# One table of attention biases for four heads, with the slope carried by the queries

## The chip, the cores and the metric

The kernel runs on one core of one Trainium2 chip. The metric is device time in microseconds (us), the median of several runs. Engines: PE is TensorE (PEld its weight loads), DVE VectorE, ACT ScalarE, POOL GpSimd, SP the engine whose queue issues every DMA of this kernel.

## The reference, cut to what matters

One layer of a hybrid decoder trunk: RMSNorm, one input projection to 13 slices of 256 columns, four token mixers side by side (dilated attention, spatial gating, pooling, retention), gates, one output projection, a second RMSNorm and the residual. Sequence 2048, width 1024, float32. The change touches the attention mixer: four heads of 64 channels, each with three branches of dilation 1, 4 and 16. A query sees itself and 128 earlier positions at the branch's step.

```python
def _alibi_slopes(n):
    return jnp.exp2(-8.0 * (jnp.arange(n, dtype=jnp.float32) + 1.0) / n)
...
    scores = jnp.einsum('bhrnqd,bhrnkd->bhrnqk', qb, kc).astype(jnp.float32) * (hd ** -0.5)
...
    band = (dist >= 0) & (dist <= window // dil)
...
    bias = -slopes[:, None, None, None, None] * (dist * dil).astype(jnp.float32)
    scores = jnp.where(mask, scores + bias, -jnp.inf)
```

With four heads the slopes are 1/4, 1/16, 1/64 and 1/256. The three branches are joined with weights from their softmax denominators.

## The kernel before, in words

**First part (lines 144 to 528).** Two halves of 1024 tokens. Each half normalises and transposes its tokens, then goes through the 13 slices. Every float32 operand is split into a high and a low part of type float32r, and each product takes three matmuls. `weights(col, n)` loads the columns of one slice (L245, tile `raw`, two buffers), copies them to the high part on ACT (L246) and subtracts that from `raw` on DVE or POOL for the low part (L247). For n = 128 it makes one copy and one subtraction of 128x1024; three such weights can be alive. `a_qk(0, e, gs)` projects the queries of head pair e and writes both parts to DRAM (`qk_d`); it runs for e = 0 and 1 in each half, so four times.

**Attention (lines 547 to 710).** `attention(0)` does heads 0 and 1, `attention(1)` heads 2 and 3. A head loads its queries `q2` and its keys `k2a`, `k2b` (L557 to L561), its bias table `tab` (L562, L563: 128x640 float32, 320 KB, one buffer) and, per branch, values `att_v` (L570 to L575). These tiles of 2048 columns share seven buffers of the tag `m8`; `tab` has one of its own. The branches come in the order 4, 16, 1. A branch takes blocks of 128 queries: two matmuls per block into `ps_s` (L626, L627), one DVE instruction that adds the table, scales and takes the row's minimum of the negated scores (L632), the exponential on ACT with the row sum (L634), transposes on PE into `ps_pt`, a split into high and low (L641 ACT, L642 DVE), two matmuls with the values into `ps_o`, and the sum of the two halves of that bank (L656 ACT, L657 DVE). At a branch's end its row statistics go to DRAM; after a head's third branch `weigh(h)` reads them back and writes the branches' weights (`fd`).

```python
            tab = pm.tile([P, T_HEAD], F32, tag="tab", bufs=1, name="tab")
            D.dma_start(tab, catt[:, h * T_HEAD:(h + 1) * T_HEAD])
...
                V.tensor_tensor_reduce(out=pr[:, u, :w], in0=ps[:, u, :w], in1=bb, scale=-(HD ** -0.5), scalar=3e38,
                                       op0=ALU.add, op1=ALU.min, accum_out=neg)
```

**Beside and after it.** `combine(0)` reads the weights of heads 0 and 1 (`fb`, L756), multiplies and adds the branches on DVE and POOL (L759 to L763) and stores the result; it stands in program order between the two calls of `attention`. Nine `partial(t)` tiles multiply the other three mixers by their output weights (`ps_out`, 36 matmuls each) while `attention(1)` and its surroundings run; `tc.issue_after` sets the earliest place of each. Then `combine(1)` and sixteen `final(t)` tiles: the rest of the output projection, norm, residual, store.

**What sets the order.** The program is traced in the order of the code. A planner then simulates it with estimated costs and writes out each engine's instruction order once, before the launch; on the chip each engine keeps to that order and waits where an input is late. SP's queue is one of these orders.

Of the kernel before, what the change touches and what calls it, by code (L numbers as in the profile page):

```python
# [9 lines left out]
F32 = mybir.dt.float32  # L10
# [3 lines left out]
AF = mybir.ActivationFunctionType  # L14
ALU = mybir.AluOpType
# [3 lines left out]
P = 128  # L19
# [6 lines left out]
HD = 64  # L26
# [4 lines left out]
COL = {n: i * 256 for i, n in enumerate(  # L31
    ("aq", "ak", "av", "ag", "bu", "bv", "bg", "cx", "cg", "dq", "dk", "dv", "dg"))}

C_ID, C_DEC, C_ZETA, C_XI, C_CD, C_INVP, C_CNT, C_MIX = 0, 128, 640, 896, 1152, 1408, 1410, 1442
T_1, T_4, T_16, T_HEAD = 0, 256, 512, 640
MASKED = 1e30
PB = {"part": 1, "fin": 8}
# [29 lines left out]
def attention_tables():  # L67

    f = np.float32
    tab = np.zeros((P, 4, T_HEAD), f)  # L70
    pos = np.arange(P)
    p1 = 16 * (pos % 8) + pos // 8
    p4 = 4 * (8 * (pos // 32) + pos % 8) + (pos // 8) % 4
    c4 = 4 * (pos % 32) + pos // 32
    k1 = np.concatenate([c4, P + c4])
    k4 = np.arange(2 * P)
    slopes = np.exp2(f(-8.0) * (np.arange(4, dtype=f) + f(1.0)) / f(4.0)).astype(f)
    for h in range(4):
        for off, qi, ki, dil in ((T_1, p1, k1, 1), (T_4, p4, k4, 4), (T_16, pos, P + pos, 16)):
            dist = qi[:, None] + P - ki[None, :]  # L80
            band = (dist >= 0) & (dist <= P)
            tab[:, h, off:off + len(ki)] = np.where(band, -slopes[h] * f(HD ** 0.5) * (dist * dil).astype(f), f(-MASKED))
    return tab.reshape(P, 4 * T_HEAD)


@with_exitstack
def hymba(ctx: ExitStack, tc: tile.TileContext, x, pre_g, w_in, sgu_g, sgu_w, sgu_b, pool_w,
# [4 lines left out]
    def r32(ap):  # L92
        return ap.bitcast(F32)
# [50 lines left out]
    with ExitStack() as c1:  # L144
# [88 lines left out]

        w_src = w_in[0].rearrange("(k p) e -> p k e", p=P)

        def weights(col, n, eng=V):

            if n == P:
                w = p1.tile([P, 2, KT, n], F32R, tag="w128", bufs=3, name="w128")
            else:  # L240
                w = pa.tile([P, 2, KT, n], F32R, tag="w256", bufs=1, name="w256")
            kc = KT * P // n
            for k in range(0, KT, kc):
                raw = p1.tile([P, kc, n], F32, tag="raw", bufs=2, name="raw")
                D.dma_start(raw, w_src[:, k:k + kc, col:col + n])  # L245
                A.activation(w[:, 0, k:k + kc], raw, AF.Copy)  # L246
                eng.tensor_tensor(w[:, 1, k:k + kc], raw, r32(w[:, 0, k:k + kc]), ALU.subtract)  # L247
            return w

        def proj_t(w, g):  # L250
# [52 lines left out]
                                    r32(vt[:, j]).rearrange("p h l d -> p h (l d)"))  # L303

        def a_qk(which, e, gs):
            w = weights(COL["aq" if which == 0 else "ak"] + e * P, P)
            for g in gs:
                ps = proj_t(w, g)
                hl = p1.tile([P, 2, GRP], F32R, tag="ys", bufs=2, name="qk_s")
                if which == 0:  # L310
                    ps, hi, lo = by_token(ps), blocked(hl[:, 0]), blocked(hl[:, 1])
                else:
                    ps, hi, lo = ps.rearrange("p (t c) -> p t c", c=4), by_chain(hl[:, 0]), by_chain(hl[:, 1])
                A.activation(hi, ps, AF.Copy)
                V.tensor_tensor(lo, ps, r32(hi), ALU.subtract)
                D.dma_start(qk_d[which][e][:, :, g * GRP:(g + 1) * GRP], r32(hl))
# [227 lines left out]

    marks = []

    def attention(p):
        o01 = (big if p == 0 else po).tile([P, 2, SEQ], F32, tag="big" if p == 0 else "o01", name="att_o01")
        o = [o01[:, 0], o01[:, 1], po.tile([P, SEQ], F32, tag="o2", name="att_o2")]
        for s in range(2):  # L550
            h = 2 * p + s
            rows = slice(s * HD, (s + 1) * HD)
            other = slice((1 - s) * HD, (2 - s) * HD)
            q2 = pm.tile([P, SEQ], F32R, tag="m8", bufs=7, name="q2")
            k2a = pm.tile([P, SEQ], F32R, tag="m8", bufs=7, name="k2a")
            k2b = pm.tile([P, SEQ], F32R, tag="m8", bufs=7, name="k2b")
            D.dma_start(r32(q2[rows]), qk_d[0][p][rows, 0])  # L557
            D.dma_start(r32(q2[other]), qk_d[0][p][rows, 1])
            for z in (rows, other):
                D.dma_start(r32(k2a[z]), qk_d[1][p][rows, 0])  # L560
                D.dma_start(r32(k2b[z]), qk_d[1][p][rows, 1])  # L561
            tab = pm.tile([P, T_HEAD], F32, tag="tab", bufs=1, name="tab")  # L562
            D.dma_start(tab, catt[:, h * T_HEAD:(h + 1) * T_HEAD])  # L563
            for b, dil in enumerate(DILS):
                vt = pm.tile([P, 16, 2 * HD], F32R, tag="m8", bufs=7, name="att_v")
                dst = r32(vt)
                if dil == 1:
                    src = v_d[h].rearrange("(n t c) d -> c t n d", c=4, t=32)
                    for c in range(4):
                        D.dma_start(dst[c * 32:(c + 1) * 32], src[c])  # L570
                elif dil == 4:
                    D.dma_start(dst.rearrange("q (j c) d -> q j (c d)", j=4),
                                v_d[h].rearrange("(j q c) d -> q j (c d)", j=4, c=4))
                else:
                    D.dma_start(dst.rearrange("q r d -> q (r d)"), v_d[h].rearrange("(q r) d -> q (r d)", r=16))  # L575
                qb = q2
                if dil != 1:
                    qb = pm.tile([P, SEQ], F32R, tag="m8", bufs=7, name="q2b")
                    if dil == 4:
                        src = r32(q2).rearrange("p (j k c i) -> p c j k i", j=4, c=4, i=8)  # L580
                        dst = qb.rearrange("p (j c k i) -> p c j k i", j=4, c=4, i=8)
                        for c in range(4):
                            (V if c < 3 else G).tensor_copy(dst[:, c], src[:, c])
                    else:
                        V.tensor_copy(qb.rearrange("p (r w i) -> p r w i", r=16, i=8),
                                      r32(q2).rearrange("p (w r i) -> p r w i", r=16, i=8))
                st = p2.tile([P, 2, 16], F32, tag="stat", bufs=2, name="att_st")
                branch(s, dil, qb, k2a, k2b, vt, tab, o[b], st)
                keep_stats(h, b, dil, st)
            weigh(h)  # L590
        return o

    def branch(s, dil, q2, k2a, k2b, vt, tab, o, st):
        rows = slice(s * HD, (s + 1) * HD)
        other = slice((1 - s) * HD, (2 - s) * HD)
        if dil == 1:
# [20 lines left out]
        def probs(blocks):  # L617

            nb = len(blocks)
            ps = ps2.tile([P, nb, GRP // nb], F32, tag="s", bufs=N_S, name="ps_s")  # L620
            pr = p2.tile([P, nb, GRP // nb], F32, tag="pr", bufs=B_PR, name="att_p")
            res = []
            for u, (n, prev) in enumerate(blocks):
                w = (1 + prev) * P
                qs = slice(n * P, (n + 1) * P)
                mm(ps[:, u, :w], q2[:, qs], keys(k2a, n, prev), True, False)  # L626
                mm(ps[:, u, :w], q2[:, qs], keys(k2b, n, prev), False, True)  # L627
            for u, (n, prev) in enumerate(blocks):
                w = (1 + prev) * P
                bb = bias if dil == 16 or prev else bias[:, P:]  # L630
                neg = st[:, 0, n:n + 1]
                V.tensor_tensor_reduce(out=pr[:, u, :w], in0=ps[:, u, :w], in1=bb, scale=-(HD ** -0.5), scalar=3e38,  # L632
                                       op0=ALU.add, op1=ALU.min, accum_out=neg)
                A.activation(pr[:, u, :w], pr[:, u, :w], AF.Exp, bias=neg, scale=-1.0, accum_out=st[:, 1, n:n + 1])  # L634
                res.append(pr[:, u, :w])
            return res
# [32 lines left out]
        if dil == 16:  # L669
            for n in range(0, 16, 4):  # L670
# [4 lines left out]
                hi, lo = split(pt, GRP)  # L675
# [171 lines left out]
    with ExitStack() as c2:  # L847
        pm = c2.enter_context(tc.tile_pool(name="pm", bufs=1, reuse_waits="tile"))
        p2 = c2.enter_context(tc.tile_pool(name="p2", bufs=1, reuse_waits="tile"))
        ps2 = c2.enter_context(tc.tile_pool(name="ps2", bufs=2, space=PSUM, reuse_waits="tile"))  # L850
        o = attention(0)
        for i in (1, 2, 3):
            out_weights(i, V if i == 2 else G)
        combine(0, o, p2, 2, False, 256, range(0, SEQ, 256))
        o = attention(1)
        for t in range(npart):
            with tc.issue_after(marks[int(len(marks) * (t + spread[0]) / npart * spread[1])]):
                partial(t)
        out_weights(0, G)
# [45 lines left out]
```

## Time and profile before

| | |
|---|---|
| median of 3 runs | 1071.59 us |
| range of the runs | 1070.7 to 1071.6 us |
| the profiled execution: its own time | 1067.77 us |
| span of that execution's profile | 1066.1 us |
| PE busy | 991.5 us, 93% of the span |
| mean granted PE clock, share of full speed | 0.972 |
| first to last instruction on `tab` (L632) | 679.2 to 917.0 us |

The span runs from the first to the last instruction of one execution; the times in the rows count from its start. Busy time is the sum of an engine's instructions; matmuls overlap, so a busy PE is not PE at its peak. A number in square brackets at the end of a timeline row is the idle time of that engine just before, and what ended it.

### The profile page before, as it was taken

The numbers are of one execution on the slowest core, as the hardware profiler recorded it, in microseconds if no ns is written. First come the engines' busy times: TensorE is split into PE (matmuls) and PEld (weight loads), VectorE is DVE, ScalarE is ACT, GpSimd is POOL, SyncE is SP. The second block draws the span as 40 slices with busy tenths as digits, with TensorE's granted clock in tenths as the row PEclk, the third lists the DMA queues.
The fourth block names the chain that finished last, engine by engine and source line by source line (L and its number), as shares of the span: only waits on it lengthen the run. The fifth ranks groups of instructions, "written<-read, shape, count | busy, mean of one in ns | idle before, by whom it ended". The sixth has DMA issues, their size and how long they took to land.

```text
span 1066.1 us, 15681 instructions
## 1 busy us (share of the span) xinstructions
PE 991.5 (93%) x5916; PEld 855.1 (80%) x5916; DVE 532.9 (50%) x1543; ACT 379.7 (36%) x847; POOL 189.6 (18%) x195
## 2 busy tenths in 40 slices
PE   5999999999999999999999999979998889987992
PEld 5889898988877988989897877868987769865781
DVE  7611216696332421023763321467676557627887
ACT  6320222131222420222211111698875548703231
POOL 2310012211232000002220124112114341222000
PEclk9999999999999999999999999989999899998996
DMA  7530313233223331142211930585656963484876
GB/s 275 150 99 21 101 58 115 84 120 95 83 79 99 99 100 40 29 129 80 80 41 50 235 97 29 152 215 150 153 172 141 222 204 78 130 248 114 271 255 218
DMA packets 120394, 136.26 MB, mean 128 GB/s; under 512 B 14976, under 2 KB 96000, under 8 KB 118272
## 3 DMA queue, kind: packets, MB, share of 16 engines
q1 hardware_dynamic: 120320, 135.28, 43.2%
q8 instruction: 46, 0.75, 0.3%
q14 instruction: 28, 0.23, 0.1%
HBM read 98.78 MB, written 36.47 MB: 127 GB/s over the span
## 4 chain that ended last, share of the span: by engine, by line
PE 70%; DMA 15%; DVE 8%; issue 3%; ACT 2%; SPq 1%; POOL 1%; DVEq 0%; ACTq 0%
PE ps_t L96 38%; PE ps_m L96 15%; PE ps_out L96 4%; DMA fb<-fd 4%; PE ps_s L96 3%; PE ps_o L96 3%; PE ps_pt L99 2%; DMA tab<-in_catt_dram 2%; PE ps_of L96 2%; DMA out_dram<-z 2%; DMA z<-partd 2%; DMA cm<-in_cmix_dram 1%; DMA partd<-z 1%; PE ps_in L96 1%; DMA ya<-ya 1%
## 5 line engine op out<-in xcount | busy, mean ns | idle before, releaser
L96 PE MATMUL ps_t<-hh,w 128*128 128x512 f32 x1152 | 368.9, 397 | 0.0
L96 PEld LDWEIGHTS ps_t<-hh,w 128*128 128x128 f32 x1152 | 216.2, 188 | 48.9 <-issue 3.4
L96 PE MATMUL ps_t<-hl,w 128*128 128x512 f32 x576 | 227.0, 394 | 0.0
L96 PE MATMUL ps_m<-w,hh 128*128 128x256 f32 x1024 | 183.6, 282 | 2.4 <-ACT hh L231 2.4
L96 PEld LDWEIGHTS ps_m<-w,hh 128*128 128x128 f32 x1024 | 157.5, 190 | 4.4 <-ACT hh L231 3.4
L96 PE MATMUL ps_out<-wo,yt 128*128 128x512 f32 x576 | 150.9, 408 | 3.7 <-DVE z L829 2.2
L96 PE MATMUL ps_m<-w,hl 128*128 128x256 f32 x512 | 145.5, 284 | 0.2 <-DVE hl L232 0.2
L96 PEld LDWEIGHTS ps_out<-wo,yt 128*128 128x128 f32 x576 | 108.4, 195 | 26.9 <-issue 3.9
L247 DVE TENSOR_TENSOR w<-raw,w 128x1024 fp32r<-128x1024 f32 x46 | 63.5, 1386 | 132.6 <-ACT w L246 132.5
L96 PEld LDWEIGHTS ps_t<-hl,w 128*128 128x128 f32 x576 | 108.4, 188 | 24.1 <-issue 1.4
L96 PEld LDWEIGHTS ps_m<-w,hl 128*128 128x128 f32 x512 | 97.8, 191 | 0.8 <-DVE hl L232 0.4
L634 ACT ACTIVATE att_p<-att_p,att_st 128x128 f32<-128x128 f32 (+1 forms) x192 | 86.5, 453 | 32.0 <-DVE att_st L632 31.7
L246 ACT ACTIVATE w<-raw 128x1024 fp32r<-128x1024 f32 x52 | 54.7, 1059 | 70.2 <-PE ps_t L96 37.6
L632 DVE CUSTOM_DVE_ANT_0 att_p<-ps_s,tab 128x128 f32<-128x128 f32 (+1 forms) x192 | 60.5, 358 | 31.4 <-PE ps_s L96 22.5
L96 PE MATMUL ps_o<-pt_lo,att_v 128*128 128x128 f32 (+1 forms) x204 | 53.9, 300 | 7.2 <-DVE pt_lo L642 7.1
L99 PE MATMUL ps_pt<-ident,att_p 128*128 128x128 f32 x300 | 53.7, 290 | 4.4 <-ACT att_p L634 4.3
L96 PE MATMUL ps_o<-pt_hi,att_v 128*128 128x128 f32 (+1 forms) x204 | 54.4, 288 | 2.4 <-DVE att_o L657 1.9
L642 DVE TENSOR_TENSOR pt_lo<-ps_pt,pt_hi 128x512 fp32r<-128x512 f32 x80 | 51.4, 651 | 5.5 <-ACT pt_hi L641 4.5
L96 PEld LDWEIGHTS ps_o<-pt_lo,att_v 128*128 128x128 f32 x204 | 41.2, 203 | 10.3 <-DVE pt_lo L642 9.5
L641 ACT ACTIVATE pt_hi<-ps_pt 128x512 fp32r<-128x512 f32 x80 | 44.3, 564 | 5.3 <-PE ps_o L96 3.4
L96 PEld LDWEIGHTS ps_o<-pt_hi,att_v 128*128 128x128 f32 x204 | 41.4, 203 | 4.8 <-issue 1.4
L657 DVE TENSOR_TENSOR att_o<-ps_o,att_o 64x512 f32<-64x512 f32 x48 | 32.9, 685 | 20.0 <-ACT att_o L656 19.5
(159 smaller groups left out, 1311.8 us busy)
## 6 DMA issues: line engine op xcount, KB each, us to landing
raw<-in_w_in_dram SPq DMA_DIRECT2D x52, 512.0 KB
qk<-qk_s SPq DMA_DIRECT2D x16, 512.0 KB
att_v<-vd SPq DMA_DIRECT2D x8, 1024.0 KB
xr<-in_x_dram SPq DMA_DIRECT2D x16, 512.0 KB
out_dram<-z SPq DMA_DIRECT2D x15, 512.0 KB
xt<-in_x_dram SPq DMA_DIRECT2D x7, 1024.0 KB
yraw<-yb SPq DMA_DIRECT2D x16, 384.0 KB
partd<-z SPq DMA_DIRECT2D x9, 512.0 KB
```

The source lines that it names most:

```text
L96: return T.matmul(o, lhsT, rhs, start=start, stop=stop, skip_group_check=True)
L99: T.transpose(o, i, ident[:n, :n])
L246: A.activation(w[:, 0, k:k + kc], raw, AF.Copy)
L247: eng.tensor_tensor(w[:, 1, k:k + kc], raw, r32(w[:, 0, k:k + kc]), ALU.subtract)
L632: V.tensor_tensor_reduce(out=pr[:, u, :w], in0=ps[:, u, :w], in1=bb, scale=-(HD ** -0.5), scalar=3e38, op0=ALU.add, op1=ALU.min, accum_out ...
L634: A.activation(pr[:, u, :w], pr[:, u, :w], AF.Exp, bias=neg, scale=-1.0, accum_out=st[:, 1, n:n + 1])
L641: A.activation(hi, pt[:, :w], AF.Copy)
L642: V.tensor_tensor(lo, pt[:, :w], r32(hi), ALU.subtract)
L657: V.tensor_tensor(dst, b0, dst, ALU.add)
```

## The change

The table is built once for slope 1 (128x640 instead of 128x2560 in DRAM) and loaded once, ahead of `attention(0)`. The query weights of head h are multiplied by the inverse of its slope (4, 16, 64 or 256), so that `ps_s` holds the scores divided by the slope; the scale of L632 becomes the slope times the old one. All factors are powers of two. In `weights`, the two heads of a pair have different factors, so the copy and the subtraction are done for each half of the columns: two ACT copies and two DVE `scalar_tensor_tensor` of 128x512 (eight runs of 64 columns) instead of one of each of 128x1024. `branch` gets the head's number instead of its place in the pair.

```diff
+SLOPES = tuple(2.0 ** -(2 * (h + 1)) for h in range(4))
...
-            tab[:, h, off:off + len(ki)] = np.where(band, -slopes[h] * f(HD ** 0.5) * (dist * dil).astype(f), f(-MASKED))
+        tab[:, off:off + len(ki)] = np.where(band, -f(HD ** 0.5) * (dist * dil).astype(f), f(-MASKED))
...
-        def weights(col, n, eng=V):
+        def weights(col, n, eng=V, scales=(1.0,)):
...
-                A.activation(w[:, 0, k:k + kc], raw, AF.Copy)
-                eng.tensor_tensor(w[:, 1, k:k + kc], raw, r32(w[:, 0, k:k + kc]), ALU.subtract)
+                for i, sc in enumerate(scales):
+                    cs = slice(i * n // len(scales), (i + 1) * n // len(scales))
+                    hi, lo = w[:, 0, k:k + kc, cs], w[:, 1, k:k + kc, cs]
+                    A.activation(hi, raw[:, :, cs], AF.Copy, scale=sc)
+                    if sc == 1.0:
+                        eng.tensor_tensor(lo, raw[:, :, cs], r32(hi), ALU.subtract)
+                    else:
+                        V.scalar_tensor_tensor(lo, raw[:, :, cs], sc, r32(hi), ALU.mult, ALU.subtract)
...
-            w = weights(COL["aq" if which == 0 else "ak"] + e * P, P)
+            if which == 0:
+                w = weights(COL["aq"] + e * P, P, scales=[1.0 / SLOPES[2 * e + s] for s in range(2)])
+            else:
+                w = weights(COL["ak"] + e * P, P)
...
-    def attention(p):
+    def attention(p, tab):
...
-            tab = pm.tile([P, T_HEAD], F32, tag="tab", bufs=1, name="tab")
-            D.dma_start(tab, catt[:, h * T_HEAD:(h + 1) * T_HEAD])
...
-                V.tensor_tensor_reduce(out=pr[:, u, :w], in0=ps[:, u, :w], in1=bb, scale=-(HD ** -0.5), scalar=3e38,
+                V.tensor_tensor_reduce(out=pr[:, u, :w], in0=ps[:, u, :w], in1=bb, scale=-SLOPES[h] * HD ** -0.5, scalar=3e38,
...
-        o = attention(0)
+        tab = pm.tile([P, T_HEAD], F32, name="tab")
+        D.dma_start(tab, catt)
+        o = attention(0, tab)
...
-        o = attention(1)
+        o = attention(1, tab)
```

## Rows read from the trace of the kernel before

**Rows 1.** The page's engine totals, and its chain that ended last, by line.

```profile
PE 991.5 (93%) x5916; PEld 855.1 (80%) x5916; DVE 532.9 (50%) x1543; ACT 379.7 (36%) x847; POOL 189.6 (18%) x195
PE ps_t L96 38%; PE ps_m L96 15%; PE ps_out L96 4%; DMA fb<-fd 4%; PE ps_s L96 3%; PE ps_o L96 3%; PE ps_pt L99 2%; DMA tab<-in_catt_dram 2%; PE ps_of L96 2%; DMA out_dram<-z 2%; DMA z<-partd 2%; DMA cm<-in_cmix_dram 1%; DMA partd<-z 1%; PE ps_in L96 1%; DMA ya<-ya 1%
```

**Rows 2.** Windows: length, PE, PEld, DVE, ACT, POOL busy (count), PEclk, DMA share, GB/s.

```profile
700.00:726.00 26.00, 18.27 (x111) 16.68 (x111) 16.05 (x50) 22.11 (x67) 0.61 (x1) 0.74 0.80 216
...
776.00:800.00 24.00, 22.07 (x154) 20.00 (x153) 16.74 (x57) 17.33 (x51) 4.08 (x4) 1.00 0.51 162
...
844.00:874.00 30.00, 21.48 (x97) 17.47 (x98) 16.22 (x52) 11.44 (x37) 12.08 (x15) 0.83 0.79 240
874.00:922.00 48.00, 47.68 (x335) 43.70 (x334) 37.89 (x125) 40.51 (x122) 6.81 (x9) 1.00 0.29 80
```

**Rows 3.** SP's queue in order of time: start, duration, line, transfer.

```profile
593.08 0.59 SPq L563 DMA_DIRECT2D tab<-in_catt_dram  x1
...
604.27 0.37 SPq L245 DMA_DIRECT2D raw<-in_w_in_dram  x1
...
775.29 0.34 SPq L563 DMA_DIRECT2D tab<-in_catt_dram  x1
...
856.04 0.41 SPq L563 DMA_DIRECT2D tab<-in_catt_dram  x1
```

**Rows 4.** DVE's timeline: first reduction of heads 0 to 3, and what precedes the last.

```profile
679.18 0.29 DVE L632 CUSTOM_DVE_ANT_0 att_p<-ps_s,tab 128x128 f32<-128x128 f32 x1 [14.31 <-PE ps_s L96]
...
722.39 0.29 DVE L632 CUSTOM_DVE_ANT_0 att_p<-ps_s,tab 128x128 f32<-128x128 f32 x1 [4.98 <-PE ps_pt L99]
...
786.53 0.29 DVE L632 CUSTOM_DVE_ANT_0 att_p<-ps_s,tab 128x128 f32<-128x128 f32 x1 [2.99 <-DMA tab<-in_catt_dram]
...
865.23 0.43 DVE L761 TENSOR_TENSOR fb<-fb,att_o 128x256 f32<-128x256 f32 x1 [9.08 <-DMA fb<-fd]
866.27 0.29 DVE L632 CUSTOM_DVE_ANT_0 att_p<-ps_s,tab 128x128 f32<-128x128 f32 x1 [0.61 <-DMA tab<-in_catt_dram]
```

**Rows 5.** PE's timeline at the three changes of head.

```profile
718.30 0.44 PE L96 MATMUL ps_s<-k2b,q2b 128*128 128x128 f32 x1 [1.76 <-DMA k2b<-qk]
...
780.13 0.28 PE L96 MATMUL ps_s<-k2b,q2b 128*128 128x256 f32 x1
...
782.18 3.05 PE L96 MATMUL ps_out<-wo,yt 128*128 128x512 f32 x12
...
848.06 0.58 PE L96 MATMUL ps_o<-pt_lo,att_v 128*128 128x256 f32 x1 [4.33 <-DVE pt_lo L642]
...
854.85 0.28 PE L96 MATMUL ps_s<-k2b,q2b 128*128 128x256 f32 x1
...
855.59 4.46 PE L96 MATMUL ps_out<-wo,yt 128*128 128x512 f32 x18
860.83 2.81 PE L96 MATMUL ps_out<-wo,yt 128*128 128x512 f32 x11 [0.78 <-ACT z L810]
867.15 0.34 PE L99 MATMUL ps_pt<-ident,att_p 128*128 128x128 f32 x1 [3.51 <-ACT att_p L634]
...
868.90 2.02 PE L96 MATMUL ps_out<-wo,yt 128*128 128x512 f32 x4
```

**Rows 6.** Groups by line and shape: busy us, mean ns, then idle time before.

```profile
L247 DVE TENSOR_TENSOR w<-raw,w 128x1024 fp32r<-128x1024 f32 x46 | 63.5, 1386 | 132.6 <-ACT w L246 132.5
L246 ACT ACTIVATE w<-raw 128x1024 fp32r<-128x1024 f32 x52 | 54.7, 1059 | 70.2 <-PE ps_t L96 37.6 <-DMA raw<-in_w_in_dram 22.7 <-issue 9.8
L402 DVE SCALAR_TENSOR_TENSOR c_pl<-c_s,cm,c_x 128x512 f32<-128x512 f32 x8 | 6.0, 749 | 23.6 <-POOL c_s L399 23.6
L383 ACT ACTIVATE c_x<-ps_t 128x512 f32<-128x512 f32 x8 | 4.8, 596 | 30.4 <-PE ps_t L96 30.4
```

**Rows 7.** ACT's second copy of query weights (first half); their first matmuls in the chain.

```profile
84.28 1.06 ACT L246 ACTIVATE w<-raw 128x1024 fp32r<-128x1024 f32 x1 [9.79 <-issue]
...
116.67 10.99 PE ps_t L96 x48
```

More of the change, by code (lines that the diff above doesn't have):

```diff
@@ L69, in attention_tables @@
     f = np.float32
-    tab = np.zeros((P, 4, T_HEAD), f)
+    tab = np.zeros((P, T_HEAD), f)
     pos = np.arange(P)
@@ L76, in attention_tables @@
     k4 = np.arange(2 * P)
[L77 to L81, printed above, removed]
-            tab[:, h, off:off + len(ki)] = np.where(band, -slopes[h] * f(HD ** 0.5) * (dist * dil).astype(f), f(-MASKED))
-    return tab.reshape(P, 4 * T_HEAD)
+    for off, qi, ki, dil in ((T_1, p1, k1, 1), (T_4, p4, k4, 4), (T_16, pos, P + pos, 16)):
+        dist = qi[:, None] + P - ki[None, :]
+        band = (dist >= 0) & (dist <= P)
+        tab[:, off:off + len(ki)] = np.where(band, -f(HD ** 0.5) * (dist * dil).astype(f), f(-MASKED))
+    return tab
 @with_exitstack
@@ L587, in attention @@
                 st = p2.tile([P, 2, 16], F32, tag="stat", bufs=2, name="att_st")
-                branch(s, dil, qb, k2a, k2b, vt, tab, o[b], st)
+                branch(h, dil, qb, k2a, k2b, vt, tab, o[b], st)
                 keep_stats(h, b, dil, st)
@@ L591, in attention, with branch @@
         return o
-    def branch(s, dil, q2, k2a, k2b, vt, tab, o, st):
+    def branch(h, dil, q2, k2a, k2b, vt, tab, o, st):
+        s = h % 2
         rows = slice(s * HD, (s + 1) * HD)
```

## The prediction

> **What bounds the kernel now.** I read the page first. Its totals show PE busy for 93% of the span with no other engine above half, and its chain is mostly projection matmuls on PE; the load of the bias table, four transfers of 320 KB, holds 2% of that chain, about 20 us [rows 1]. That share is what the change can reach, so the next view is the attention by windows. Between 844 and 874 us PE is busy for 21.48 of 30 us at a mean granted clock of 0.83; between 776 and 800 it is busy for 22.07 of 24; from 874 to 922 for 47.68 of 48 [rows 2]. The reader is to see that two changes of head look alike in the chain and differ for PE: one leaves it idle, the other doesn't. The queue of SP shows why the table is late: head 0's load is issued at 593.08, far ahead, but heads 2 and 3 issue theirs at 775.29 and 856.04, when the head before has read the one buffer for the last time [rows 3]. DVE's timeline shows the first reduction that needs each table: 679.18, 722.39, 786.53 and 866.27 [rows 4]. PE's timeline shows when the scores for it lay ready, and what PE did meanwhile [rows 5].
>
> **What it costs in the first part.** Four calls of `weights` change. Each has one ACT copy of 1059 ns and one DVE subtraction of 1386 ns; after the change it has two copies and two subtractions of half the size. The nearest rows of that size are an ACT copy of 128x512 at 596 ns and a DVE scalar_tensor_tensor of 128x512 at 749 ns [rows 6]. So ACT pays 2 x 596 - 1059 = 133 ns and DVE 2 x 749 - 1386 = 112 ns more per call, 1.0 us in all for the four. A strided row of 64 elements is not in the trace; if it doubled each of the new instructions the sum would be 4 x (133 + 1192 + 112 + 1498) ns = 11.7 us of engine time. Neither is on the path: the second query weights of the first half are copied at 84.28 and even the first set's matmuls begin only at 116.67 [rows 7], so there are some 30 us of PE work in front. The second half has the same pattern. I take nothing, and 1.0 us if that cover were gone.
>
> [...]
>
> **The table's one load** is now issued ahead of the queries of head 0. Before, it was the seventh transfer of that head, at 593.08, and its first use comes at 679.18 [rows 3, 4]. It moves in front of the six half-loads of `q2`, `k2a` and `k2b`; these have over 80 us in hand. It also sits at the start of its pool, so the other tiles there shift by 2560 bytes per partition and may lie over other tiles of the first part, which are released at other times. Queued behind those loads on SP is the raw weight load at 604.27. If the loads ahead of it were held, that one, the weights made of it and PE would be late in turn. SP's order around 593 would have to stand still for some 11 us, until 604.27, before that load is late at all; I take nothing here, and a longer hold would cost what it exceeds.
>
> **The three later loads go.** Their wait goes with them, and what is late next decides the gain.
>
> Head 1: the reduction starts at 722.39. The last of the keys for it arrives for the matmul at 718.30, which takes 0.44 [rows 5]; from 718.7 it is 3.7 us to the reduction, and that much is the most that it could come sooner. The wait is shown as one for PE; that the table was its true end is a reading. PE's 700 to 726 has 7.7 us idle, but the wait shown in it is one for keys [rows 2, 5]. Between 0 and 3.7 I take 1.0, nearer to the end where PE waits for keys anyway.
>
> Head 2: the scores are ready at 780.13 + 0.28 = 780.4, the reduction comes at 786.53, so 6.1 us [rows 4, 5]. PE, however, meanwhile runs the projection of a partial tile (12 matmuls in 3.05 us at 782.18, for one) and is busy for 22.07 of 24 us [rows 2, 5]. That work has to be done at some point. Bounds 0 and 6.1; I take 0, since PE is the bound here.
>
> Head 3: the scores are ready at 854.85 + 0.28 = 855.1, the reduction comes at 866.27, so 11.1 us. PE covers the first part with 18 + 11 matmuls of partial tiles, which end at 860.83 + 2.81 = 863.64, then has nothing until 867.15: 3.51 us idle. [...] From 867.15 to 870.92 that is 3.77 us at half speed, a loss of 1.9. Together 5.4 us [rows 5].
> But the row in front of that reduction is a multiplication of `combine(0)` that itself waited 9.08 us, until 865.23, for the branch weights `fb` [rows 4]. In today's DVE order the table would release only the 0.6 us after it; with 320 KB less in the queue at 240 GB/s [rows 2], 1.4 us, at most about 2.0. The order is written anew, though. With the table's wait in the plan the multiplication could well come first; without it the reduction is ready at 855.1, long before `fb`. So 5.4 is what I take, with 0.6 as the lower end.
>
> From 874 to 922 PE is fully busy [rows 2], so what is gained before it reaches the end of the attention, and with it the last `weigh`, `combine(1)` and the final tiles.
>
> Sum: 0 + 0 + 1.0 + 0 + 5.4 = 6.4 us less. Of the profiled execution's 1067.8 that leaves 1061.4. The runs' median is 1071.6, 0.36% above that execution; the same 6.4 us off it gives 1065.2 us.
>
> **The rivals.** (a) The waits go but something else ends last. For it: at head 3 DVE is held by `fb` to within 1.0 us of the reduction, and at head 2 PE is covered. Against it: the DVE order is not kept. Gain 0.6 to 2.0, so 1069.6 to 1071.0.
>
> (b) More than the idle time at the table comes back. The partial tiles' matmuls that now stand in front of the waits at heads 2 and 3 (12 and 29, so 3.0 and 7.3 us by 0.25 each) are free to fill other holes, such as the one of 4.33 us at 848.06 [rows 5]. With head 2's whole 6.1 as well this gives 6.4 + 6.1 = 12.5, so 1059.1. Against it: their earliest places are fixed by `issue_after`, and partial work at a wait is already well placed.
>
> (c) Slower, by the multiplications of `combine(0)`. DVE follows a fixed order, and the one at 865.23 sat for 9.08 us behind a transfer that the planner had expected sooner; all reductions, splits and sums behind it on DVE wait too, and PE for these. Today most of that wait lies in the same time as the table's, and PE has 29 matmuls to cover it. If the new order puts it in front of a reduction where PE has no such cover, PE loses up to 9.1 us and another 1.9 at the lower clock as at head 3, against the gain of 6.4: 4.6 us over, 1076.2. It decides from the point where the uncovered part exceeds 6.4 - 1.9 = 4.5 us. The hole at 848.06, 4.33 us behind a DVE instruction, shows that it happens [rows 5].
>
> (d) The change does nothing measurable because the planner keeps its order and PE's total work, the bound, is the same: this has the numbers of (a) and is counted there.
>
> **How the numbers follow.** A change within 0.2%, 2.1 us, is about what a measurement of this kernel can't tell from none. Forecast 0.47, with a range of its own of 1061 to 1069; (a) 0.20, all within 0.2%; (b) 0.15; (c) 0.18, of which 0.16 is slower by over 0.2% and 0.02 within. That gives faster 0.62, same 0.22, slower 0.16. The range reaches from (b) to (c), 1058 to 1076.5; what spreads beyond these two, and what none of them describes, is the 2 in 10 left out.
>
> **What would show it right or wrong.** Right: one DMA of the table, near 589, and none later; the first reduction of head 3 within about 1 us of its last score matmul and in front of the `fb` multiplication in DVE's order; the 3.51 us hole at 867 gone, a clock near 1.0 there, and an attention that ends some 6 us sooner against the first part's end; four pairs of half-size copies some 30 us ahead of their matmuls, with the first part unchanged to within 1 us. Wrong: DVE waits for `fb` with reductions behind it and PE idle there; new waits for `k2b` or `att_v` at the changes of head; SP held near 590 to 605 and a gap in the projections after it; or a strided half-size copy on the path.

## The result, and the profile after

The changed kernel takes 1064.44 us (median of 7 runs, 1056.98 to 1067.62) against 1071.57 for the kernel before (7 runs, 1069.94 to 1074.65): ratio 0.9924, interval 0.9900 to 0.9949. That is 7.1 us less, where 6.4 were forecast. The sum came out; two of the terms under it did not.

A caution for the two traces: the profiled execution of the changed kernel took 1066.84 us, near the slow end of its runs, and that of before 1067.77, faster than all of its timed runs. This pair shows 1 us of the 7. Stage by stage I therefore also use the first experiment, whose orders on PE, DVE, ACT and POOL are the same as the changed kernel's, line for line, and whose profiled execution took 1060.96 us.

The page of the changed kernel, its totals and its chain by line, against [rows 1]:

```profile
PE 993.5 (93%) x5916; PEld 855.0 (80%) x5916; DVE 540.4 (51%) x1547; ACT 379.6 (36%) x851; POOL 190.9 (18%) x195
...
PE ps_t L95 7%; PE ps_out L95 5%; PE ps_o L95 3%; DMA fb<-fd 3%; PE ps_s L95 2%; PE ps_pt L98 2%; DMA k2b<-qk 2%; DMA partd<-z 1%; DVE att_p L639 1%; DVE z L850 1%; DMA sga<-agd 1%; DMA att_v<-vd 1%; DMA out_dram<-z 1%; DVE pt_lo L649 1%; DMA yraw<-yb 1%
```

The table is gone from the chain, PE's work is the same. `fb` (3%) and `k2b` (2%) stand in it. This chain could be followed back for 42% of the span only, so its shares can't be set against those of [rows 1]; the first experiment's is followed over the whole span and has no table either, with `fb` at 5% and `k2b` at 2%. SP's queue in the changed kernel, against [rows 3]:

```profile
589.74 0.52 SPq L859 DMA_DIRECT2D tab<-in_catt_dram  x1
...
608.18 0.37 SPq L244 DMA_DIRECT2D raw<-in_w_in_dram  x1
```

One load, near 589 as forecast. DVE's timeline in the changed kernel, against [rows 4]:

```profile
683.88 0.29 DVE L639 CUSTOM_DVE_ANT_0 att_p<-ps_s,tab 128x128 f32<-128x128 f32 x1 [14.31 <-PE ps_s L95]
...
723.72 0.29 DVE L639 CUSTOM_DVE_ANT_0 att_p<-ps_s,tab 128x128 f32<-128x128 f32 x1 [5.42 <-PE ps_s L95]
...
781.53 0.29 DVE L639 CUSTOM_DVE_ANT_0 att_p<-ps_s,tab 128x128 f32<-128x128 f32 x1 [0.62 <-PE ps_s L95]
...
846.21 0.43 DVE L768 TENSOR_TENSOR fb<-fb,att_o 128x256 f32<-128x256 f32 x1 [4.97 <-DMA fb<-fd]
...
853.31 0.26 DVE L639 CUSTOM_DVE_ANT_0 att_p<-ps_s,tab 128x128 f32<-128x128 f32 x1
...
866.09 0.43 DVE L768 TENSOR_TENSOR fb<-fb,att_o 128x256 f32<-128x256 f32 x1 [2.84 <-DMA fb<-fd]
```

No reduction waits for the table any more. Head 0's reduction is 4.7 us later than before, heads 2 and 3 start 5.0 and 13.0 us sooner. DVE still waits for `fb`, now in shorter pieces on both sides of head 3's first reduction. PE at that change of head, against the 3.51 us of [rows 5]:

```profile
847.29 0.40 PE L98 MATMUL ps_st<-ident,att_st 128*32 128x128 f32 x1 [3.67 <-DVE pt_lo L649]
...
853.98 0.48 PE L95 MATMUL ps_s<-k2a,q2b 128*128 128x128 f32 x1 [3.16 <-DVE att_st L639]
```

Windows of the changed kernel, in the columns of [rows 2]:

```profile
844.00:874.00 30.00, 20.33 (x89) 16.36 (x90) 20.16 (x53) 9.59 (x34) 15.22 (x18) 0.77 0.69 186
874.00:922.00 48.00, 47.26 (x316) 43.16 (x315) 35.58 (x114) 38.14 (x110) 8.11 (x12) 0.93 0.29 74
```

The hole at head 3 did not close. It became two, of 3.67 and 3.16 us, both ended by DVE: the first while DVE waited 4.97 us for `fb`, the second while it waited 1.12 us more and worked through `combine(0)`'s instructions. The mean granted clock of the stretch is 0.77 where it was 0.83.

So the seven microseconds must show elsewhere. Cut the span after the first part at the last write of branch weights (`fd`), and take PE alone. The kernel before, all PE work in the attention (679.18 to 928.75) and in the final stage (to the end); under it `ps_out`, the output projection, alone (columns: length, PE busy, clock, DMA share, GB/s):

```profile
679.18:928.75 249.57, 223.55 (x1439) 0.94 0.63 165
928.75:1066.10 137.35, 104.12 (x430) 0.90 0.70 223
...
679.18:928.75 249.57, 92.63 (x339) 0.94 0.63 165
928.75:1066.10 137.35, 104.12 (x430) 0.90 0.70 223
```

The same stages with the changed kernel's order, in the trace of the first experiment:

```profile
679.16:923.35 244.19, 216.54 (x1411) 0.93 0.65 162
923.35:1059.20 135.85, 109.86 (x459) 0.92 0.73 231
...
679.16:923.35 244.19, 88.12 (x311) 0.93 0.65 162
923.35:1059.20 135.85, 109.86 (x459) 0.92 0.73 231
```

Length minus busy is PE's idle time. In the attention it did not fall: 249.57 - 223.55 = 26.0 before, 244.19 - 216.54 = 27.7 in the first experiment. The attention is 5.4 us shorter because 28 matmuls of partial tiles (339 less 311) are no longer in it. They stand in the final stage, which grew by 5.7 us of PE work and yet is 1.5 us shorter: its idle time fell from 137.35 - 104.12 = 33.2 to 26.0. Much of that idle time lies behind PE's last matmuls, in the kernel before and in the first experiment:

```profile
1044.47 0.85 PE L96 MATMUL ps_out<-wo,ysa 128*128 128x512 f32 x3
```

```profile
1039.24 0.85 PE L95 MATMUL ps_out<-wo,ysa 128*128 128x512 f32 x3
```

From there to the end it is 20.7 and 19.1 us; what lies between matmuls fell from 12.5 to 6.9. What PE waited for there, in the kernel before (us in total, times, longest):

```profile
PE ps_out L96 <- ACT ysa L769: 7.5, 2, 4.9
PE ps_out L96 <- DVE z L829: 2.2, 1, 2.2
PE ps_out L96 <- DVE ysa L770: 1.9, 1, 1.9
```

and with the changed kernel's order, in the first experiment:

```profile
PE ps_out L95 <- ACT ysa L778: 3.3, 1, 3.3
PE ps_out L95 <- DVE yt L800: 3.2, 3, 1.7
PE ps_out L95 <- DVE ysa L779: 0.4, 1, 0.4
```

`ysa` is the result of `combine(1)`, which can't begin before the attention ends. In this pair the wait for it fell from 9.4 to 3.7 us: matmuls that don't need the attention were left over to put in front of it. This one wait scatters, though: with the very same order on every engine it was 5.9 us in experiment five and 8.2 in experiment eleven. The idle time of the whole stage is the safer figure, and the account below goes by that.

### The profile page after: what moved, and what is told of

The parts are those of the page before. It is cut to its first block, busy times and chain, and to the rows that moved or that the text cites. A ratio compares the mean times of both kernels' runs of the same rounds, so it can differ in the third digit from the quotient of the medians.

```text
span 1065.1 us, 15690 instructions
## 1 busy us (share of the span) xinstructions
PE 993.5 (93%) x5916; PEld 855.0 (80%) x5916; DVE 540.4 (51%) x1547; ACT 379.6 (36%) x851; POOL 190.9 (18%) x195
## 5 line engine op out<-in xcount | busy, mean ns | idle before, releaser
L95 PE MATMUL ps_out<-wo,yt 128*128 128x512 f32 x576 | 155.6, 414 | 6.1 <-DVE yt L798 3.1
L250 DVE TENSOR_TENSOR w<-raw,w 128x1024 fp32r<-128x1024 f32 x42 | 59.0, 1412 | 109.6 <-ACT w L248 109.4
L248 ACT ACTIVATE w<-raw 128x1024 fp32r<-128x1024 f32 (+1 forms) x56 | 55.0, 997 | 70.1 <-PE ps_t L95 37.6
L649 DVE TENSOR_TENSOR pt_lo<-ps_pt,pt_hi 128x512 fp32r<-128x512 f32 x80 | 51.2, 650 | 12.5 <-ACT pt_hi L648 12.1
L98 PE MATMUL ps_pt<-ident,att_p 128*128 128x128 f32 x300 | 51.2, 283 | 0.8 <-ACT att_p L641 0.8
L95 PEld LDWEIGHTS ps_o<-pt_hi,att_v 128*128 128x128 f32 x204 | 40.8, 200 | 9.5 <-DVE att_o L664 4.6
L648 ACT ACTIVATE pt_hi<-ps_pt 128x512 fp32r<-128x512 f32 x80 | 44.1, 563 | 11.2 <-PE ps_pt L98 5.7
L95 PE MATMUL ps_s<-k2a,q2b 128*128 128x128 f32 (+1 forms) x128 | 37.5, 325 | 8.6 <-DMA k2a<-qk 4.4
```

Of the source, the lines that this page charges most:

```text
L95: return T.matmul(o, lhsT, rhs, start=start, stop=stop, skip_group_check=True)
L98: T.transpose(o, i, ident[:n, :n])
L248: A.activation(hi, raw[:, :, cs], AF.Copy, scale=sc)
L250: eng.tensor_tensor(lo, raw[:, :, cs], r32(hi), ALU.subtract)
L648: A.activation(hi, pt[:, :w], AF.Copy)
L649: V.tensor_tensor(lo, pt[:, :w], r32(hi), ALU.subtract)
```

## The experiments

In each heading the median and the ratio to the kernel before, run on the same chip, with its interval. Where two orders are called the same, the instructions of an engine agree one by one in both traces, in operation, tiles and shape.

**One: the changed kernel with its load in the old place. 1062.65 us, 0.9914 (0.9897 to 0.9932).**

```diff
         tab = pm.tile([P, T_HEAD], F32, name="tab")
-        D.dma_start(tab, catt)
         o = attention(0, tab)
...
                 D.dma_start(r32(k2b[z]), qk_d[1][p][rows, 1])
+            if h == 0:
+                D.dma_start(tab, catt)
```

> The changed kernel, but the one table load stands in head 0 behind its queries and keys, where the first load stood before. Theory A (the table's waits at the changes of head are what was gained; the load's new place in front of the queries costs some 4 us in the first part): first reduction back from 683.9 to about 679.5 us, head distances as in the changed kernel, median near 1064.4 - 4 = 1060 us. Rival B (the gain comes from an order written anew, and any edit shuffles it): anything between 1060 and 1072, with no tie to the first reduction. Rival C (the first part's loss is given back at the end anyway, since PE is the bound there): first reduction near 679.5, median still 1063 to 1066.

The interval overlaps the changed kernel's, so the place of the load is worth nothing that these runs can tell (the medians differ by 1.8 us). First reductions of heads 1 to 3 in this trace:

```profile
719.09 0.29 DVE L641 CUSTOM_DVE_ANT_0 att_p<-ps_s,tab 128x128 f32<-128x128 f32 x1 [5.49 <-PE ps_s L95]
...
776.84 0.29 DVE L641 CUSTOM_DVE_ANT_0 att_p<-ps_s,tab 128x128 f32<-128x128 f32 x1 [0.72 <-PE ps_s L95]
...
848.81 0.27 DVE L641 CUSTOM_DVE_ANT_0 att_p<-ps_s,tab 128x128 f32<-128x128 f32 x1
```

Head 0 starts at 679.16, as before at 679.18 [rows 4]. The lead over before is 3.3 us at head 1, 9.7 at head 2, 17.5 at head 3, and 5.4 at the last `fd`: most of what is won at the heads is gone when the attention ends.

**Two: the kernel before, its table loaded once, no scaling. 1063.05 us, 0.9916 (0.9902 to 0.9930).**

```diff
-            tab = pm.tile([P, T_HEAD], F32, tag="tab", bufs=1, name="tab")
-            D.dma_start(tab, catt[:, h * T_HEAD:(h + 1) * T_HEAD])
+            if h == 0:
+                D.dma_start(tab, catt[:, :T_HEAD])
```

> The kernel before with head 0's table loaded once, in its old place, and used for all four heads (the biases of heads 1 to 3 are left out: they get head 0's); no scaling of the query weights. Theory A: the same as e1, within 2 us, since only the loads matter: about 1060 us. Rival B: between 1060 and 1072, not tied to e1. If the split of the query weights cost anything, this one would be faster than e1 by that.

This kernel leaves out the biases of heads 1 to 3, and the whole gain is here without a line of the scaling. It comes from the loads that are gone. PE's order is the changed kernel's.

**Three: the scaled queries, but the table loaded again for each head. 1069.82 us, 0.9985 (0.9969 to 1.0001).**

```diff
-        tab = pm.tile([P, T_HEAD], F32, name="tab")
-        D.dma_start(tab, catt)
...
+            tab = pm.tile([P, T_HEAD], F32, tag="tab", bufs=1, name="tab")
+            D.dma_start(tab, catt)
```

> The changed kernel's query scaling with the one table of slope 1, but loaded again for every head into one buffer, as before. Theory A: as the kernel before, 1071.6 us within 2 us, first reductions at about 679, 722, 786 and 866 us. Rival B (any edit shuffles the order): off by 3 us or more, either way. The copies and subtractions of the query weights: four pairs of 128x512 more, some 30 us ahead of their matmuls, no gap on PE.

The counterpart of the second: scaling alone gives and costs nothing that these runs can tell. PE's order is that of the kernel before.

**Four: the kernel before, with head 0's load ahead of its queries. 1072.05 us, 1.0003 (0.9990 to 1.0017).**

```diff
+            if h == 0:
+                tab = pm.tile([P, T_HEAD], F32, tag="tab", bufs=1, name="tab")
+                D.dma_start(tab, catt[:, :T_HEAD])
```

> The kernel before with only head 0's table load moved in front of its queries, as in the changed kernel; the other three loads and their waits stay. Theory A: queries of head 0 land later, DVE's copies of them stand in front of work of the first part, the first reduction moves from 679.2 to about 683.5 us, and the time from 1071.6 to about 1075.5. Rival: the place of the load costs nothing and the first part's 4.7 us come from the scaling or from other tiles' places: first reduction at 679.2, 1071.6 us.

No cost in time. The first reduction comes at 681.43 us in this trace, between the two theories, but what precedes it on SP's queue is late by as much. The theory that the early load explains the later start of head 0 in the changed kernel's trace falls.

**Five: the changed kernel again. 1064.43 us, 0.9926 (0.9902 to 0.9950).**

> The changed kernel once more, beside the next three, for a second trace. It differs from e1 in nothing but the place of one DMA in SP's order. If that place costs the first part 4.7 us each time: first reduction at 683 to 684 us and a median 3 to 5 us above e1's 1062.7. If the 4.7 us were one execution's late transfer: first reduction within 1.5 us of e1's 679.2, median within 2 us of e1's.

Head 0 starts at 680.7 this time, not 683.88. In the changed kernel's first trace, DVE's cast of head 0's queries stood for 9.44 us until they had come, and held the gating slice's work behind it, for which PE waited 2.32 us; its timelines:

```profile
603.29 1.51 DVE L589 CAST q2b<-q 128x512 fp32r<-128x512 f32 x3 [9.44 <-DMA q<-qk]
...
606.59 0.51 PE L95 MATMUL ps_t<-hh,w 128*128 128x512 f32 x1 [2.32 <-DVE b_t L370]
```

In this second trace the cast waits 6.19 us and PE not at all:

```profile
601.07 1.51 DVE L589 CAST q2b<-q 128x512 fp32r<-128x512 f32 x3 [6.19 <-DMA q<-qk]
```

With the same order in both, that is a transfer late in one execution, not the change.

**Six to eight: the changed kernel with one reload.** The first experiment's load, and a second one at head 1, or with `(0, 2)` and `(0, 3)` at head 2 or 3.

```diff
+            if h in (0, 1):
+                tab = pm.tile([P, T_HEAD], F32, tag="tab", bufs=1, name="tab")
+                D.dma_start(tab, catt)
```

> e1, but the same table is loaded a second time for head 1, into the one buffer, so that the wait at the change from head 0 to head 1 is back and the other two stay away. The prediction's sizes (1.0 us at head 1, 0 at head 2, 5.4 at head 3): 1063.7 us. Rival (each wait counts by how much earlier its reduction came, 3.4 of 17.7 us): 1062.7 + 1.9 = 1064.6.

> e1 with a second load for head 2 alone. The prediction's sizes: 0, so 1062.7 us, since PE is covered by partial tiles there. Rival (by how much earlier the reduction came, 6.3 of 17.7): 1066.1.

> e1 with a second load for head 3 alone. The prediction's sizes: 5.4, so 1068.1 us, with PE idle some 3.5 us around 867 at a lower clock. Rival (8.0 of 17.7): 1067.0; rival (behind it DVE waits for the branch weights anyway): 1063 to 1064.

Head 1: 1068.11 us, 0.9967 (0.9950 to 0.9984). Head 2: 1065.33, 0.9939 (0.9920 to 0.9958). Head 3: 1061.39, 0.9913 (0.9882 to 0.9944). Against the 1062.65 of the first that is 5.4 more, 2.7 more (the intervals overlap a little) and 1.3 less, which is nothing. Against experiment five, the changed kernel run beside these three, it is 3.7 more, 0.9 more and 3.0 less. So head 1 has a price of some 4 to 5 us, head 2 one that these runs hardly tell from none, head 3 none. The forecast had 1.0, 0 and 5.4. The first reduction after the reload, in the three traces:

```profile
724.52 0.29 DVE L642 CUSTOM_DVE_ANT_0 att_p<-ps_s,tab 128x128 f32<-128x128 f32 x1 [4.76 <-PE ps_pt L98]
```

```profile
784.69 0.29 DVE L642 CUSTOM_DVE_ANT_0 att_p<-ps_s,tab 128x128 f32<-128x128 f32 x1 [1.38 <-DMA tab<-in_catt_dram]
```

```profile
855.61 0.26 DVE L642 CUSTOM_DVE_ANT_0 att_p<-ps_s,tab 128x128 f32<-128x128 f32 x1
```

The middle one shows a wait of 1.38 us for the table. In the dearest the profile names a transpose into `ps_pt`, which the reduction doesn't read; what it waits for is found by setting its last score matmul against the first experiment's, where PE's order is the same up to there (first experiment, then the reload at head 1):

```profile
718.08 0.44 PE L95 MATMUL ps_s<-k2b,q2b 128*128 128x128 f32 x1 [1.84 <-DMA k2b<-qk]
```

```profile
720.61 0.44 PE L95 MATMUL ps_s<-k2b,q2b 128*128 128x128 f32 x1 [1.74 <-DMA k2b<-qk]
```

With no load the reduction comes 1.0 us after that matmul's start (719.09), with the load 3.9 us after it, and the trace has the table's last packet landing at 724.38, 0.14 us ahead of the reduction. So the table holds it for some 2.9 us. In the kernel before it is 4.1 us (718.30 to 722.39), so 3.1 us go to the table. Head 3's reload lands in time because SP issues it at 843.47, 12 us ahead of its reduction:

```profile
843.47 1.39 SPq L572 DMA_DIRECT2D tab<-in_catt_dram  x1
```

So the wait left on the chip falls with the price: some 2.9 us, 1.38 and none. PE's order goes with it too. With the reload at head 3 it is the first experiment's, all 5916 matmuls; with those at heads 1 and 2 the planner wrote another, from the reload on. The runs don't separate wait and order. The final stages (windows from the last `fd`, head 1, 2 and 3, each from its own trace; columns as above):

```profile
931.88:1063.20 131.32, 99.93 (x420) 0.91 0.73 225
```

```profile
930.69:1060.10 129.41, 101.53 (x425) 0.91 0.72 228
```

```profile
929.31:1064.20 134.89, 109.15 (x459) 0.92 0.72 231
```

Idle 31.4, 27.9 and 25.7 us, next to 26.0 with no reload. The first two left 420 and 425 matmuls for that stage, the third 459, as many as with no reload. These traces don't show the prices themselves: head 1's is of the shortest of its twelve executions (1064.93 us), head 3's of one near its longest (1065.96 of 1057.91 to 1067.80). With the reload at head 1 the mean granted clock was 0.976 in that execution and 0.968 in the median of the twelve, where the first experiment's six had 0.971 to 0.975; so some of head 1's price can lie in the clock.

**Nine and ten: no partial tiles.** The kernel before, and the first experiment, each with `npart=0`; all sixteen tiles are then done in the final stage.

```diff
-          ..., npart=9, spread=(0.3, 0.95)):
+          ..., npart=0, spread=(0.3, 0.95)):
```

> The kernel before without partial tiles in the attention (npart 0: all sixteen tiles are projected in full at the end). PE has nothing to cover the table's waits with. Slower than 1072 us, by how much is open (the work of 324 matmuls, some 75 us, moves behind the attention, and the attention gets shorter by less than that). It is the partner of the next run: theory D (the lead at head 3's start, 17.5 us in the trace, is given back because partial tiles that had covered the waits are only moved behind): the next run is 14 us or more faster than this one. Rival E (it is given back by something else in the last head): 8 to 10 us faster, as with partial tiles.

> e1 without partial tiles in the attention. Theory D: 14 us or more faster than the run before this one, and the lead at the last reduction about as large as at head 3's first. Rival E: 8 to 10 us faster.

1112.64 us, 1.0381 (1.0363 to 1.0399), with four loads; 1112.16 us, 1.0378 (1.0361 to 1.0395), with one. Both theories had the single load win 8 us or more here. It wins nothing. With four loads, heads 2 and 3 start so:

```profile
772.85 0.29 DVE L632 CUSTOM_DVE_ANT_0 att_p<-ps_s,tab 128x128 f32<-128x128 f32 x1 [6.93 <-PE ps_s L96]
...
824.68 0.27 DVE L632 CUSTOM_DVE_ANT_0 att_p<-ps_s,tab 128x128 f32<-128x128 f32 x1
```

The table is no longer what these two reductions wait for, though its loads are issued at 762.04 and 814.01, 10.8 and 10.7 us ahead of them, much as before (11.2 and 10.2 by [rows 3, 4]). They land at 772.48 and 824.06, after 10.4 and 10.1 us where it was 11.2 and 10.2, so they are hardly faster; the rest is that the reductions' other conditions come later. Head 1's table is still late: its reduction comes 43.4 us after head 0's, with one load 40.8. The two attention stages, four loads and then one:

```profile
678.77:914.71 235.94, 163.66 (x1123) 0.81 0.58 143
```

```profile
680.00:915.66 235.66, 167.81 (x1123) 0.80 0.57 139
```

They are equally long, and PE is idle for some 70 us in each. Without partial tiles the loads cost nothing, though head 1's wait is there. That fits a price that lies in where partial tiles are put; at heads 2 and 3, where the tables are in time, this pair doesn't tell what a wait costs that nothing covers.

**Eleven: the first experiment with the partial tiles due earlier. 1062.64 us, 0.9916 (0.9890 to 0.9941).**

```diff
-          npart=9, spread=(0.3, 0.95)):
+          npart=9, spread=(0.3, 0.8)):
```

> e1 with the earliest places of the partial tiles drawn towards the front (spread 0.3 to 0.8 instead of 0.95), so that fewer of them stand in front of the last head's statistics. If the 17.4 us from the last reduction to the last weights (11.8 before) are partial tiles' work put in front of a chain that sets the end: 12 us there and a median near 1058. Theory D in its strict form (PE is the bound, work only moves): 1061 to 1064.

The same time, and the same order as the first experiment's on every engine, the transfers on SP's queue included. An earlier permission did not move the work, so this run says nothing of what moving it would bring. It is a repeat of the first, and shows what one order scatters by:

```profile
923.92:1061.41 137.49, 108.33 (x459) 0.93 0.72 228
```

The final stage idles for 29.2 us here and for 26.0 there. The 27.9 with the reload at head 2 is within that; the 31.4 at head 1 and the 33.2 before are outside it.

**Twelve: the first experiment with `combine(0)`'s DVE instructions on POOL. 1058.92 us, 0.9888 (0.9870 to 0.9906).**

The two additions and the gate of each piece move like the multiplication shown.

```diff
+            W = V if keep else G
-            V.tensor_tensor(fb[:, 0], fb[:, 0], o[0][:, cs], ALU.mult)
+            W.tensor_tensor(fb[:, 0], fb[:, 0], o[0][:, cs], ALU.mult)
...
```

> e1 with the multiplications and additions of combine(0) on POOL instead of DVE, so that no reduction or split stands behind a wait for the branch weights. If rival (c) of the prediction holds part of the time (DVE waits 5, 1 and 3 us for fb between 841 and 866 in the changed kernel, with PE idle behind the first): 1056 to 1060 us. If PE has work meanwhile or POOL becomes late with the partial tiles' casts: 1062 us or more.

3.7 us less than the first, with intervals that meet only between 0.9897 and 0.9906, and as much less than experiment eleven, run beside it. POOL and DVE in its trace:

```profile
807.76 0.74 POOL L768 TENSOR_TENSOR fb<-fb,att_o 128x256 f32<-128x256 f32 x1 [13.77 <-DMA fb<-fd]
```

```profile
836.17 0.29 DVE L641 CUSTOM_DVE_ANT_0 att_p<-ps_s,tab 128x128 f32<-128x128 f32 x1 [2.69 <-PE ps_s L95]
```

POOL now sits behind `fb` for 13.77 us, in a run that is shorter all the same, and head 3 begins 157.4 us after head 0, where it was 169.7 in the first experiment. Of these 12 us the end keeps about 4. The edit takes 32 instructions off DVE along with the wait, and PE's order is a new one, so the three are not told apart. Its final stage:

```profile
932.31:1057.12 124.81, 99.00 (x415) 0.91 0.75 236
```

That is 25.8 us idle, as in the first experiment, with fewer matmuls left than in the kernel before (415 against 430). So matmuls left over are not the only way to a short wait there.

## Why the prediction was right, and where not

- **First part, 0: right.** Experiments two and three show no cost of the scaling that can be measured. The rows of the changed kernel:

```profile
L252 DVE SCALAR_TENSOR_TENSOR w<-raw,w 128x512 fp32r<-128x512 f32 x8 | 5.2, 688 | 22.0 <-ACT w L248 22.0
...
L248 ACT ACTIVATE w<-raw 128x512 fp32r<-128x512 f32 x8 | 4.6, 624 | 18.7 <-issue 9.4 <-PE ps_t L95 9.3
```

  ACT pays 2 x 624 - 1059 = 189 ns per call (133 forecast), DVE 2 x 688 - 1386 = -10 ns (112 forecast). Rows of 64 strided elements did not double anything: DVE's 688 ns are below the nearest row's 749, ACT's 624 are 28 above its 596 [rows 6]. That DVE pays nothing holds against the mean alone: the 1386 is over 46 subtractions some of which ran longer (their median is 1226, the longest 2591), and by that median the split costs 2 x 688 - 1226 = 150 ns.
- **The one load's place, 0: right.** Experiments one, four and five show no cost of it. The reason given was wrong for the queries: they had not "over 80 us in hand". DVE's cast reads them some 10 us after their issue, and in the kernel before it already waits for them:

```profile
599.87 1.51 DVE L583 CAST q2b<-q 128x512 fp32r<-128x512 f32 x3 [6.50 <-DMA q<-qk]
```

  In one execution of the changed kernel that wait grew to 9.44 us and PE idled for 2.32 behind it.
- **Head 1, 1.0: under-sized.** Putting its reload back costs 5.4 us by the first experiment, 3.7 by the fifth. The upper bound was 3.7; the wait for the table is some 3 us of it, so the reading that the table was its true end was right. What failed is the choice of 1.0 "where PE waits for keys anyway": that PE waits for keys there did not make the reload cheap. What takes the price to or past the whole wait, the new order or the clock, is open.
- **Head 2, 0: not refuted.** It measured 2.7 us by the first experiment and 0.9 by the fifth, at the edge of what the runs tell apart. That PE was covered there by matmuls of partial tiles was read rightly. Whether covered means free at this head stays open; that such matmuls are missed later is read from the stages, not from this run.
- **Head 3, 5.4: wrong, it is nothing.** The step that failed is "5.4 is what I take", which needed the reduction to get in front of the `fb` multiplications and PE's idle time to go with it. The reduction did start 13 us sooner, but PE's hole only moved to other DVE instructions queued behind `fb`, as the warning sign in the prediction had it. The 1.9 in the sum is half speed from 867.15 to 870.92: the granted clock was 0.55 there in the kernel before, but no run shows those 1.9 us won back. In the changed kernel it was 0.50 behind each of PE's two holes, from 847.29 to 850.82 and from 853.98 to 857.00. The table's lateness there was only in part the one buffer's: the head before had read it for the last time by 852.2 us, and SP issued the load 3.9 us later, behind other transfers of its queue. Experiment eight puts the load back and loses nothing. Experiment twelve took `combine(0)`'s wait and work off DVE and got 3.7 us: that speaks for the mechanism of rival (c), as a cost and not as one that makes the change slower. DVE's 9.08 us for `fb` in [rows 4] suggest that the kernel before pays it too; no run moved it there.
- **"What is gained before it reaches the end of the attention": right in size, wrong in kind.** The attention is 5.4 us shorter in the first experiment, 4.7 and 3.2 in the changed kernel's two traces. But PE's idle time in it stayed at 26 to 28 us, where the prediction had idle time going; what is gone from it is PE work, 28 matmuls. That work stands in the final stage, where it cost no time, as the idle time there fell. This is the mechanism of rival (b), free partial tiles filling other holes, with a place that I had not named and about half the size: 28 matmuls and 5.4 + 1.5 = 6.9 us over both stages, where (b) had 41 and 12.5. Rival (a), a gain of 0.6 to 2.0, is out: the interval of the ratio ends at 0.9949.

PE's order, fixed before the launch, sorts the medians of the kernels with partial tiles. With the order of the kernel before (also in experiments three and four) they are 1069.8 to 1072.3 us, with the changed kernel's (in both its runs and in experiments one, two, eight and eleven) 1061.4 to 1064.4, whether a table is loaded again, the queries are scaled, or the first load moved. The three other orders, of experiments six, seven and twelve, have 1068.1, 1065.3 and 1058.9. The final stage idles for 33.2 to 34.7 us with the first order (three traces) and for 25.7 to 29.2 with the second (six). The loads that are gone thus come with another order, and the order with the time; how much of the 7.1 us is the order and how much the waits themselves is not shown. That the shorter idle time comes from the matmuls left over is argued, and experiment twelve shows that it can be had without them. That the total came out within 1 us was luck: 5.4 us taken at head 3 that weren't there made up for head 1's, taken too small.

Open: the three reloads add up to 5.4 + 2.7 - 1.3 = 6.8 us against the first experiment and to 3.7 + 0.9 - 3.0 = 1.6 against the fifth, while all three at once cost 7.2 (experiment three less one, 1069.82 - 1062.65) or 9.7 (the kernel before run beside them, 1072.31, less one), so it isn't shown that they add. Experiment eight keeps PE's order and adds a load, at no cost, but that load came in time; what a late one costs at an unchanged order, and with it whether head 1's price is a wait of the chip or a worse order, was not tried.

## What to carry to other kernels

Where independent work fills a wait, a wait that the trace shows as covered can still have a price, as the filler may be missing at the next hole (here, with the one load, 28 matmuls more were left for the final stage, and PE idled there for 26.0 us instead of 33.2); so look for the end of the program's own uncovered wait before costing the removal at nothing. Where a planner writes the order anew, the wait seen at one place told little of what its removal brought (1.0 forecast and some 4 to 5 measured, 5.4 forecast and nothing measured): put one load back at a time, measure, and see whether the order changed with it. Where the profile names an engine that the waiting instruction doesn't read from, set the row against a run without the suspected load. And before crediting the removal of one wait, look at what else in the same in-order queue waits for a transfer: moving that second wait, and its work, to an engine with time to spare (POOL, busy for 18% of the span in the changed kernel) brought 3.7 us more, about half of what the change itself did.

## What had not been expected of the hardware

Splitting one 128x1024 subtraction on DVE into two scaled ones of 128x512 with rows of 64 elements cost 688 ns each: nothing against the mean of the whole one, 1386 ns, and 150 ns against its median, 1226. Between executions of one kernel a transfer came some 2 us later (the first queries, 603.29 against 601.07 in experiment five), and head 0's first reduction in that execution 3 us later, nearly half of what this change is worth: one pair of traces could not have shown it.
